# Seven block products for eight: Strassen's scheme in the down projection of a streaming encoder step

## The chip, the core and the metric

The kernel runs on one core of one Trainium2 chip. The metric is the device time of one execution in microseconds (us): 2781.47 us, the median of three runs (2781.33 to 2783.16).

## What is computed

One step of a hybrid encoder layer over 512 prompt tokens and 128 sample tokens (together 640 rows, five token tiles of 128), with model width 2048. The step is a long one (modulation, projections, attention, a recurrent branch, output projection, MLP); the change is in the last product of the MLP:

```python
x = x + gate_a * rmsnorm(mixed @ w_out, g_post_mix)
h = rmsnorm(x, g_pre_mlp) * (1 + scale_m) + shift_m
f = jnp.square(jax.nn.relu(h @ w_up)) @ w_down      # u = relu(.)^2, (640, 8192) ; w_down (8192, 2048)
return x + gate_m * rmsnorm(f, g_post_mlp)
```

All inputs are fp32. Every matrix product is made of three matmuls on fp32r operands: an operand is split into a high part and the rest (`hi`, `lo`), and hi\*hi + hi\*lo + lo\*hi is summed.

## The kernel before

The program is laid out by a tile scheduler: the code is written in program order with priorities (`tc.high_priority(200)` for splits and weight loads), pools give the buffers, and the scheduler fixes one order of instructions per engine. Each engine then works through its own list in order, and an instruction that waits holds back all behind it. DMAs are issued by SyncE (SP), also in order.

A split (`split_into`, L83 to L86) is one ScalarE (ACT) cast to `hi` (L85) and one VectorE (DVE) subtraction for `lo` (L86). Weights arrive as half blocks of 128x1024 fp32 (512 KB) in a ring of six buffers (tag `raw`), and their `hi` and `lo` lie in three buffers each (`PARTS = 3`).

The MLP's first product (`up_pair`, L993 to L1037) already goes by Strassen's scheme: seven products of 24 matmuls for two column tiles, with weight sums on DVE ahead of some splits (L1010, L1016, L1026, L1032). Its result u goes to DRAM, transposed, in 64 tiles `u_dr[f]` of 128 x 640.

The down projection starts at L1054. `acc` (128 x 5 x 2048, fp32) holds the result in SBUF. K = 8192 is cut into 16 blocks n of 512, the 2048 columns into four column blocks cb of 512. For each n, four tiles of u are read back and split (`up_tile`, tags `fh`, `fl`, five buffers each); for each cb the two half blocks of `w_down[n, cb]` are loaded and split, and for each of five token tiles t (`down_cols`, L1066 to L1077) 12 matmuls (4 tiles of u, 3 of hi and lo) go into one PSUM bank, which DVE then adds to `acc` (L1077; L1075 is the copy for n = 0). So one (n, cb) is 60 matmuls, two splits and five additions. The last block, n = 15, is kept apart: its weights are split into `late_h`, `late_l`, and norm, gate and output of each token tile follow its matmuls.

AH and AL are two SBUF areas (tags of the pool `act`) of 128 x 10240 fp32. In the up projection they hold the operands of its products; in the down projection they are free until `late_h` and `late_l`.

Of the kernel before, what the change touches and what calls it, by code (L numbers as in the profile page):

```python
# [19 lines left out]
P = 128  # L20
# [19 lines left out]
def stream_step(ctx: ExitStack, tc: tile.TileContext, I, O):  # L40
# [86 lines left out]

    u_dr = [dr.tile([P, T], F32, name=f"u_dr{f}") for f in range(64)]

# [600 lines left out]
    with tc.tile_pool(name="ph2", bufs=1) as pl:  # L730
# [169 lines left out]
        def up_out(c, f, half, op):  # L900

            V.scalar_tensor_tensor(out=c, in0=c, scalar=0.0, in1=c, op0=op, op1=ALU.mult)
            nc.sync.dma_start(u_dr[f][:, H2 * half : H2 * half + H2], c)

# [36 lines left out]
        def plain(j, ct, half):  # L941
# [11 lines left out]
            S.activation(c, c, AF.Square)  # L953
            nc.sync.dma_start(u_dr[2 * j + ct - 1][:, H2 * half : H2 * half + H2], c)
            yield
# [35 lines left out]
    with tc.tile_pool(name="up", bufs=1) as pl:  # L991
# [3 lines left out]
        def up_pair(j):  # L995
# [40 lines left out]
            S.activation(c, c, AF.Square)  # L1036
            nc.sync.dma_start(u_dr[2 * j][:, H2:], c)  # L1037

# [13 lines left out]


    with tc.tile_pool(name="ph3", bufs=1) as pl:  # L1054
        acc = pl.tile([P, NT, D], F32, name="acc")
        NBLK = 16

        def up_tile(f):
            with tc.high_priority(200):
                u = load(u_dr[f], f"u{f}")  # L1060
            fh = pl.tile([P, T], F32R, tag="fh", bufs=5, name=f"fh{f}")
            fl = pl.tile([P, T], F32R, tag="fl", bufs=5, name=f"fl{f}")
            split_into(fh, fl, u)
            return fh, fl

        def down_cols(n, fs, t, cb, parts, ps):  # L1066
            for kk in range(4):
                xh, xl = [x[:, P * t : P * t + P] for x in fs[kk]]
                wh, wl = cols(parts, 512 * kk, 512)
                PE.matmul(ps, xh, wh, start=kk == 0, stop=False)  # L1070
                PE.matmul(ps, xh, wl, start=False, stop=False)  # L1071
                PE.matmul(ps, xl, wh, start=False, stop=kk == 3)  # L1072
            dst = acc[:, t, 512 * cb : 512 * cb + 512]
            if n == 0:
                V.tensor_copy(dst, ps)  # L1075
            else:
                V.tensor_add(dst, dst, ps)  # L1077
# [11 lines left out]
        n = NBLK - 1  # L1089
        fs += [up_tile(4 * n + i) for i in (1, 2, 3)]  # L1090
        first = load_split(I["w_down"][n, 0], f"d{n}0")
# [28 lines left out]
        for t in range(NT):  # L1120
            down_cols(n, fs, t, 0, first, bank("s", f"dn{n}0{t}"))
        gate = [None] * 4
# [12 lines left out]
        for i, t in enumerate(order):  # L1135
            for cb in range(1, 4):
                down_cols(n, fs, t, cb, late[cb], bank("sto"[(3 * t + cb) % 3], f"dn{n}{cb}{t}"))
# [107 lines left out]
```

## Time and profile before

| what | before |
|---|---|
| median of 3 runs | 2781.47 us |
| the profiled execution | 2785.3 us, of which 2783.2 us span |
| PE (TensorE) busy | 2720.8 us, 98% |
| DVE busy | 1481.9 us, 53% |
| ACT busy | 951.0 us, 34% |
| down projection, first to last matmul | 1890.6 to 2771.7 us |

The page gives busy time by engine, then the costliest groups of instructions with the duration of one and the idle time ahead of it; the trace behind it can be asked for single stretches. A matmul's duration in the trace (390 ns) is longer than its distance to the next one, because matmuls overlap; what counts is the number in a stretch in which PE never rests. The same holds, less strongly, for DVE: an instruction that waits for nothing starts a little before the one ahead of it has ended. Names: `dn` is a bank of the down projection, `d_h`, `d_l` the split weights, `fh`, `fl` the split u.

### The profile page before, as it was taken

The numbers are of one execution on the slowest core, as the hardware profiler recorded it, in microseconds if no ns is written. First come the engines' busy times: TensorE is split into PE (matmuls) and PEld (weight loads), VectorE is DVE, ScalarE is ACT, GpSimd is POOL, SyncE is SP. The second block draws the span as 40 slices with busy tenths as digits, with TensorE's granted clock in tenths as the row PEclk, the third lists the DMA queues.
The fourth block names the chain that finished last, engine by engine and source line by source line (L and its number), as shares of the span: only waits on it lengthen the run. The fifth ranks groups of instructions, "written<-read, shape, count | busy, mean of one in ns | idle before, by whom it ended". The sixth has DMA issues, their size and how long they took to land.

```text
span 2783.2 us, 39612 instructions
## 1 busy us (share of the span) xinstructions
PE 2720.8 (98%) x15934; PEld 2331.2 (84%) x15934; DVE 1481.9 (53%) x2377; ACT 951.0 (34%) x1530; POOL 53.2 (2%) x103
## 2 busy tenths in 40 slices
PE   7999999999999989999999999999999999999998
PEld 3677787877768778899999999997888888888886
DVE  5465534435353366766666666664444544444457
ACT  4264433433353255433333333332211211121222
POOL 0000000000000011100000000000000000000000
PEclk9999999999999999999999999999999999999999
DMA  9944465665664466733333333333333332232235
GB/s 335 352 148 153 153 201 182 212 212 188 227 212 144 161 247 224 234 105 116 111 118 110 115 107 117 110 110 104 121 94 96 109 110 92 95 122 89 92 117 178
DMA packets 148279, 425.92 MB, mean 153 GB/s; under 512 B 21976, under 2 KB 48504, under 8 KB 145536
## 3 DMA queue, kind: packets, MB, share of 16 engines
q1 hardware_dynamic: 143824, 406.28, 44.3%
q0 software_dynamic: 4128, 17.04, 1.7%
q8 instruction: 125, 2.05, 0.3%
q14 instruction: 58, 0.48, 0.1%
q10 hardware_dynamic: 144, 0.07, 0.0%
HBM read 375.94 MB, written 47.40 MB: 152 GB/s over the span
## 4 chain that ended last, share of the span: by engine, by line
PE 91%; DMA 3%; issue 2%; ACT 2%; DVE 2%; POOL 0%; SPq 0%; DVEq 0%; ACTq 0%; POOLq 0%
PE dn L1071 10%; PE dn L1070 10%; PE dn L1072 10%; PE u L895 8%; PE u L896 8%; PE u L897 8%; PE wo L757 2%; PE wo L759 2%; PE wo L758 2%; PE mm_ps L142 2%; PE g_ps L142 1%; PE zx L211 1%; PE zg L211 1%; PE ma_ps L142 1%; PE zx L213 1%
## 5 line engine op out<-in xcount | busy, mean ns | idle before, releaser
L1070 PE MATMUL dn<-d_h,fh 128*128 128x512 f32 x1220 | 473.7, 390 | 5.9 <-ACT fh L85 4.4
L1071 PE MATMUL dn<-d_l,fh 128*128 128x512 f32 x1220 | 475.5, 391 | 0.0
L1072 PE MATMUL dn<-d_h,fl 128*128 128x512 f32 x1220 | 473.4, 390 | 0.0
L1077 DVE TENSOR_TENSOR acc<-acc,dn 128x512 f32<-128x512 f32 x300 | 205.8, 686 | 321.8 <-PE dn L1072 319.2
L85 ACT CAST d_h<-d_r 128x1024 fp32r<-128x1024 f32 x122 | 127.9, 1048 | 512.9 <-PE dn L1072 503.1
L1070 PEld LDWEIGHTS dn<-d_h,fh 128*128 128x128 f32 x1220 | 229.6, 188 | 54.7 <-ACT fh L85 4.7
L1071 PEld LDWEIGHTS dn<-d_l,fh 128*128 128x128 f32 x1220 | 229.5, 188 | 51.7 <-DVE d_l L86 4.2
L1072 PEld LDWEIGHTS dn<-d_h,fl 128*128 128x128 f32 x1220 | 229.5, 188 | 47.5 <-DVE fl L86 0.4
L86 DVE TENSOR_TENSOR d_l<-d_r,d_h 128x1024 fp32r<-128x1024 f32 x122 | 148.9, 1221 | 85.4 <-ACT d_h L85 85.4
L758 PE MATMUL wo<-wo_l,mix_hi 128*128 128x512 f32 x320 | 125.8, 393 | 1.4 <-DVE wo_l L86 1.4
L757 PE MATMUL wo<-wo_h,mix_hi 128*128 128x512 f32 x320 | 126.6, 396 | 0.0
L759 PE MATMUL wo<-wo_h,mix_lo 128*128 128x512 f32 x320 | 125.7, 394 | 0.0
L86 DVE TENSOR_TENSOR wo_l<-wo_r,wo_h 128x1024 fp32r<-128x1024 f32 x48 | 58.6, 1223 | 104.3 <-ACT wo_h L85 101.5
L85 ACT CAST fh<-u 128x640 fp32r<-128x640 f32 x64 | 43.9, 725 | 145.9 <-PE dn L1071 144.0
L86 DVE TENSOR_TENSOR a_l<-u,a_h 128x1024 fp32r<-128x1024 f32 x41 | 50.2, 1225 | 71.4 <-ACT a_h L85 71.4
L85 ACT CAST wo_h<-wo_r 128x1024 fp32r<-128x1024 f32 x48 | 50.1, 1051 | 111.7 <-PE wo L759 99.6
L757 PEld LDWEIGHTS wo<-wo_h,mix_hi 128*128 128x128 f32 x320 | 60.6, 190 | 16.4 <-issue 3.6
L211 PE MATMUL zg<-h_hi,zg_h 128*128 128x320 f32 x224 | 73.9, 330 | 0.0
L211 PE MATMUL zx<-h_hi,zx_h 128*128 128x320 f32 x224 | 73.7, 329 | 0.0
L895 PE MATMUL u<-mix_hi,g_h 128*128 128x320 f32 x232 | 71.8, 309 | 1.6 <-DVE p L1028 1.6
L758 PEld LDWEIGHTS wo<-wo_l,mix_hi 128*128 128x128 f32 x320 | 60.6, 190 | 13.8 <-DVE wo_l L86 1.8
L897 PE MATMUL u<-mix_hi,g_l 128*128 128x320 f32 x232 | 71.7, 309 | 0.0
(1730 smaller groups left out, 6647.5 us busy)
## 6 DMA issues: line engine op xcount, KB each, us to landing
u<-in_w_up_dram SPq DMA_DIRECT2D x140, 512.0 KB
d_r<-in_w_down_dram SPq DMA_DIRECT2D x122, 512.0 KB
ma<-in_w_mod_dram SPq DMA_DIRECT2D x64, 512.0 KB
mm<-in_w_mod_dram SPq DMA_DIRECT2D x64, 512.0 KB
g<-in_w_mod_dram SPq DMA_DIRECT2D x64, 512.0 KB
wo_r<-in_w_out_dram SPq DMA_DIRECT2D x48, 512.0 KB
u<-u_dr SPq DMA_DIRECT2D x64, 320.0 KB
u_dr<-c SPq DMA_DIRECT2D x87, 160.0 KB
```

Of the source, the lines that this page charges most:

```text
L85: S.copy(hi, raw)
L86: V.tensor_sub(lo, raw, hi.bitcast(F32))
L211: PE.matmul(out, lh, AH[:, k, t], start=first, stop=False)
L757: PE.matmul(ps, xh, wh, start=first, stop=False)
L758: PE.matmul(ps, xh, wl, start=False, stop=False)
L895: PE.matmul(out, hi[:, c], xh[:, k, :], start=first and k == 0, stop=False, skip_group_check=True)
L896: PE.matmul(out, hi[:, c], xl[:, k, :], start=False, stop=False, skip_group_check=True)
L897: mm = PE.matmul(out, lo[:, c], xh[:, k, :], start=False, stop=k == 7, skip_group_check=True)
L1070: PE.matmul(ps, xh, wh, start=kk == 0, stop=False)
L1071: PE.matmul(ps, xh, wl, start=False, stop=False)
L1072: PE.matmul(ps, xl, wh, start=False, stop=kk == 3)
L1077: V.tensor_add(dst, dst, ps)
```

## The change

Blocks n = 0 to 14 are taken in eight groups: group 0 is block 0 alone, with its 512 values of K cut in two; groups 1 to 7 are pairs of blocks (n, n + 1), each of which is one half of K. The 512 prompt tokens are cut into two halves of 256, and the columns into the block cb and the block cb + 2. A group makes two passes (`columns`, cb = 0 and 1). In each pass, seven products (1, 2, 5, 6, 3, 7, 4, in this order) take the place of the eight of a two by two block product, on sums and differences of blocks of u and of w_down (Winograd's form). A product is, for each half h of its K (two in groups 1 to 7, one in group 0), 12 matmuls: two token tiles, two K tiles, three of hi and lo. The sample's token tile is not part of the scheme: its products are four more, 6 matmuls per h each, beside products 1, 2, 3 and 7 and on their split weights. Each product's banks are added to or subtracted from `acc` by `gather`; a bank goes on accumulating over several products.

The operands made of u are split into AH and AL (`ud_hi`, `ud_lo`, one set). During pass 1 of a group `u_operands` builds the next group's: seven of 128 x 1024 and three for the sample of 128 x 512 (in group 0 half as wide). Blocks of u are read through two buffers (`ar`) and one (`at`). u lies in DRAM in 16 tiles of 128 x 4 x 640.

```diff
-    u_dr = [dr.tile([P, T], F32, name=f"u_dr{f}") for f in range(64)]
+    u_dr = [dr.tile([P, 4, T], F32, name=f"u_dr{n}") for n in range(16)]
...
+        ORDER = (1, 2, 5, 6, 3, 7, 4)
+        AX_h = act.tile([P, 8704], F32R, tag="AH", name="ud_hi")
+        AX_l = act.tile([P, 8704], F32R, tag="AL", name="ud_lo")
+        groups = [[((0, 0), (0, 1))]] + [[((n, h), (n + 1, h)) for h in range(2)] for n in range(1, NBLK - 1, 2)]
...
+        def u_operands(g):
+            one = lambda r, t, name: u_part(g, r, 256 * t, 256, "ar", f"{name}_{g}")
+            u_split(g, 1, one(0, 0, "a11"))
+            yield
+            u_split(g, 2, one(1, 0, "a12"))
+            yield
+            x = u_part(g, 1, 256, 256, "at", f"a22_{g}")
+            V.tensor_sub(x, x, one(0, 1, "a21"))
+            u_split(g, 5, x)
+            yield
+            V.scalar_tensor_tensor(out=x, in0=x, scalar=-1.0, in1=one(0, 0, "b11"), op0=ALU.mult, op1=ALU.subtract)
+            u_split(g, 6, x)
+            yield
+            a = one(1, 0, "b12")
+            V.scalar_tensor_tensor(out=a, in0=x, scalar=-1.0, in1=a, op0=ALU.mult, op1=ALU.subtract)
+            u_split(g, 3, a)
+            yield
+            a = one(0, 0, "c11")
+            V.tensor_sub(a, a, one(0, 1, "c21"))
+            u_split(g, 7, a)
+            x1, x2 = [u_part(g, r, TP, TS, "ar", f"s{r}_{g}") for r in range(2)]
+            u_split(g, -1, x1)
+            u_split(g, -2, x2)
+            V.tensor_sub(x2, x2, x1)
+            u_split(g, -3, x2)
+            yield
+            u_split(g, 4, one(1, 1, "b22"))
+            yield
...
+        def product(g, i, raws, banks, first, name, sample=None):
+            nh = len(raws)
+            for h in range(nh):
+                with tc.high_priority(200):
+                    hi, lo = split(raws[h], f"{name}{i}{h}")
+                for p in range(2):
+                    at = place(i, h).start + P * p
+                    for kk in range(2):
+                        xs = [x[:, at + 256 * kk : at + 256 * kk + P] for x in (AX_h, AX_l)]
+                        dot(banks[p], xs, hi, lo, kk, first and h == 0 and kk == 0, h == nh - 1 and kk == 1)
+                if sample:
+                    s, ps, s_first, s_last = sample
...
+        def columns(g, cb, building):
...
+            def more(a, b):
+                with tc.high_priority(200):
+                    for x, y in zip(a, b):
+                        V.tensor_add(x, x, y)
...
+            product(g, 1, w11, b1, True, nm, (-1, y1, True, False))
+            for p in range(2):
+                gather(p, cb, b1[p], 1)
+            done()
...
+            product(g, 2, w21, b3, True, nm, (-2, y1, False, True))
...
+            more(w11, w12)
+            product(g, 5, w11, b2, True, nm)
...
+            more(w11, w22)
+            product(g, 6, w11, b1, False, nm)
...
+            product(g, 3, w22, b2, False, nm, (-3, y2, True, False))
...
+            more(w12, w22)
+            w21 = [w_half(g, h, 1, cb, "raw", "v21") for h in hs]
+            product(g, 7, w12, b1, False, nm, (-1, y2, False, True))
...
+            more(w11, w21)
+            product(g, 4, w11, b1, False, nm)
...
+        for _ in u_operands(0):
+            pass
+        for g in range(len(groups)):
+            columns(g, 0, iter(()))
+            columns(g, 1, u_operands(g + 1) if g + 1 < len(groups) else iter(()))
...
-        fs = [up_tile(0)]
-        for n in range(NBLK - 1):
-            fs += [up_tile(4 * n + i) for i in (1, 2, 3)]
-            cur, fs = fs, [up_tile(4 * n + 4)]
-            for cb in range(4):
-                parts = load_split(I["w_down"][n, cb], f"d{n}{cb}")
-                for t in range(NT):
-                    down_cols(n, cur, t, cb, parts, bank("s", f"dn{n}{cb}{t}"))
```

What the change does to the engines' lists is seen at three places. In the rows below, a name such as `d2160_l` is the low part of the weights of group 2, pass 1, product 6, half 0; `w11_210` is the block w11 of group 2, pass 1, half 0; `dn501` is the bank of n = 5, cb = 0, t = 1.

SP, where the up projection ends, before (the last stores of u, then weights):

```order
L903 DMA u_dr63_180<-c12_31_17558 128x320
L72 DMA d00_r_1024_17694<-in_w_down_dram 128x1024
L903 DMA u_dr63_180<-p5_31_17527 128x320
L1037 DMA u_dr62_179<-c21_31_17652 128x320
L72 DMA d01_r_0_17774<-in_w_down_dram 128x1024
```

The same place after:

```order
L903 DMA u_dr15_132<-c12_31_17510 128x320
L903 DMA u_dr15_132<-p5_31_17479 128x320
L1038 DMA u_dr15_132<-c21_31_17604 128x320
L1138 DMA w11_000_17668<-in_w_down_dram 128x1024
L1138 DMA w11_010_17842<-in_w_down_dram 128x1024
L1080 DMA a11_0_17616<-u_dr0_117 128x2x256
L1080 DMA a12_0_17620<-u_dr0_117 128x2x256
L1080 DMA a22_0_17624<-u_dr0_117 128x2x256
```

Before, the first tiles of u and the first two weight blocks are issued ahead of the last store (`c21_31`), in the rows shown and the ten above them; now the first weight block (`w11_000`) and the first blocks of u stand behind it, and the load of `w11_000` waits for that store's end, since its buffer lies where the up projection's pieces lay.

DVE in the middle of the stage, before (the end of n = 4 and the beginning of n = 5):

```order
L1077 TENSOR_TENSOR acc_17661<-acc_17661,dn433_19400 128x512
L86 TENSOR_TENSOR fl21_19431<-u21_19428,fh21_19430 128x640
L86 TENSOR_TENSOR fl22_19437<-u22_19434,fh22_19436 128x640
L1077 TENSOR_TENSOR acc_17661<-acc_17661,dn434_19414 128x512
L86 TENSOR_TENSOR d50_1_l_19461<-d50_r_1024_19454,d50_1_h_19460 128x1024
```

The same engine after, the splits of products 6 and 3 of group 2, pass 1 (`d2120`, `d2121` are the banks of product 5):

```order
L86 TENSOR_TENSOR d2160_l_19247<-w11_210_19082,d2160_h_19246 128x1024
L86 TENSOR_TENSOR ud_lo_17615<-a12_3_19195,ud_hi_17614 128x1024
L1173 TENSOR_TENSOR w11_210_19082<-w11_210_19082,v21_210_19339 128x1024
L86 TENSOR_TENSOR d2161_l_19263<-w11_211_19084,d2161_h_19262 128x1024
L1123 TENSOR_TENSOR acc_17613<-acc_17613,d2120_19199 128x512
L1123 TENSOR_TENSOR acc_17613<-acc_17613,d2121_19200 128x512
L1173 TENSOR_TENSOR w11_211_19084<-w11_211_19084,v21_211_19341 128x1024
L86 TENSOR_TENSOR d2130_l_19287<-w22_230_19144,d2130_h_19286 128x1024
```

Between two splits of weights there now stand a weight sum (L1173), a split of u for the group after (`ud_lo`) and the gathers (L1123).

DVE at the head of group 1, before (the end of n = 0 and the beginning of n = 1):

```order
L86 TENSOR_TENSOR d10_1_l_18053<-d10_r_1024_18046,d10_1_h_18052 128x1024
L86 TENSOR_TENSOR fl7_18035<-u7_18032,fh7_18034 128x640
L86 TENSOR_TENSOR fl8_18041<-u8_18038,fh8_18040 128x640
L1077 TENSOR_TENSOR acc_17661<-acc_17661,dn100_18056 128x512
L86 TENSOR_TENSOR d11_0_l_18131<-d11_r_0_18126,d11_0_h_18130 128x1024
```

The same place after, pass 0 of group 1, from the sixth operand to product 2's second half (`d1021_l`):

```order
L1098 SCALAR_TENSOR_TENSOR a22_1_17928<-a22_1_17928,b11_1_17954 128x1024
L1173 TENSOR_TENSOR w12_121_18119<-w12_121_18119,w22_121_18123 128x1024
L1102 SCALAR_TENSOR_TENSOR b12_1_17984<-a22_1_17928,b12_1_17984 128x1024
L86 TENSOR_TENSOR ud_lo_17615<-a22_1_17928,ud_hi_17614 128x1024
L86 TENSOR_TENSOR ud_lo_17615<-b12_1_17984,ud_hi_17614 128x1024
L1106 TENSOR_TENSOR c11_1_18017<-c11_1_18017,c21_1_18019 128x1024
L86 TENSOR_TENSOR ud_lo_17615<-c11_1_18017,ud_hi_17614 128x1024
L86 TENSOR_TENSOR ud_lo_17615<-s0_1_18024,ud_hi_17614 128x512
L86 TENSOR_TENSOR ud_lo_17615<-s1_1_18026,ud_hi_17614 128x512
L1111 TENSOR_TENSOR s1_1_18026<-s1_1_18026,s0_1_18024 128x512
L86 TENSOR_TENSOR d1021_l_18148<-w21_101_18069,d1021_h_18147 128x1024
```

For group 1 the operands' rows, from the first (`a11_1`, eleven rows further up) on, stand within its own pass 0, ahead of the second half of product 2, and not beside the pass before, as in the later groups.

## Rows read from the trace of the kernel before

**Rows 1.** The page: the span, and busy time of each engine.

```profile
span 2783.2 us, 39612 instructions
PE 2720.8 (98%) x15934; PEld 2331.2 (84%) x15934; DVE 1481.9 (53%) x2377; ACT 951.0 (34%) x1530; POOL 53.2 (2%) x103
```

**Rows 2.** Busy time by stretch: up projection, down projection, its end, its entry.

```profile
core 0: us, PE busy (x) PEld busy (x) DVE busy (x) ACT busy (x) POOL busy (x), PEclk, DMA share, GB/s
1200.00:1880.00 680.00, 680.00 (x4638) 680.00 (x4637) 442.68 (x466) 251.32 (x332) 0.00 (x0) 1.00 0.35 113
1950.00:2700.00 750.00, 750.00 (x3300) 618.04 (x3299) 353.87 (x440) 147.43 (x162) 0.00 (x0) 1.00 0.32 102
2700.00:2783.00 83.00, 70.62 (x309) 57.17 (x307) 58.84 (x100) 25.84 (x57) 0.00 (x0) 0.96 0.52 178
1884.00:1892.00 8.00, 3.59 (x18) 2.90 (x17) 2.68 (x3) 4.06 (x7) 0.00 (x0) 0.81 0.46 144
```

**Rows 3.** Waits from 2000 to 2700 us: who waited, total, times, longest.

```profile
ACT d_h L85 <- PE dn L1072: 434.8, 78, 11.2
DVE acc L1077 <- PE dn L1072: 292.5, 154, 2.0
DVE d_l L86 <- ACT d_h L85: 68.4, 39, 1.8
PEld dn L1071 <- DVE d_l L86: 3.9, 13, 0.3
```

**Rows 4.** The page's groups of instructions: busy, mean ns of one, idle before.

```profile
L1070 PE MATMUL dn<-d_h,fh 128*128 128x512 f32 x1220 | 473.7, 390 | 5.9 <-ACT fh L85 4.4
L1077 DVE TENSOR_TENSOR acc<-acc,dn 128x512 f32<-128x512 f32 x300 | 205.8, 686 | 321.8 <-PE dn L1072 319.2
L85 ACT CAST d_h<-d_r 128x1024 fp32r<-128x1024 f32 x122 | 127.9, 1048 | 512.9 <-PE dn L1072 503.1
L86 DVE TENSOR_TENSOR d_l<-d_r,d_h 128x1024 fp32r<-128x1024 f32 x122 | 148.9, 1221 | 85.4 <-ACT d_h L85 85.4
```

**Rows 5.** Timeline of PE at the entry: start, us, engine, line, instruction.

```profile
1890.57 0.80 PE L1070 MATMUL dn<-d_h,fh 128*128 128x512 f32 x1 [4.41 <-ACT fh L85]
1891.16 0.63 PE L1071 MATMUL dn<-d_l,fh 128*128 128x512 f32 x1
1891.59 0.63 PE L1072 MATMUL dn<-d_h,fl 128*128 128x512 f32 x1
...
1895.80 0.40 PE L1070 MATMUL dn<-d_h,fh 128*128 128x512 f32 x1
1896.03 0.39 PE L1071 MATMUL dn<-d_l,fh 128*128 128x512 f32 x1
```

**Rows 6.** The chain of waits at the entry, in order of time.

```profile
1887.84 1.78 DMA u_dr<-c
...
1889.79 0.73 ACT fh L85
```

**Rows 7.** Timeline of DVE in the up and the down projection.

```profile
1747.99 1.23 DVE L86 TENSOR_TENSOR a_l<-u,a_h 128x1024 fp32r<-128x1024 f32 x1 [2.25 <-ACT a_h L85]
1749.25 1.23 DVE L1010 TENSOR_TENSOR u<-u,u 128x1024 f32<-128x1024 f32 x1
1750.60 1.23 DVE L1026 TENSOR_TENSOR u<-u,u 128x1024 f32<-128x1024 f32 x1
...
2111.42 0.69 DVE L1077 TENSOR_TENSOR acc<-acc,dn 128x512 f32<-128x512 f32 x1
2112.02 1.22 DVE L86 TENSOR_TENSOR d_l<-d_r,d_h 128x1024 fp32r<-128x1024 f32 x1
2113.16 1.56 DVE L86 TENSOR_TENSOR fl<-u,fh 128x640 fp32r<-128x640 f32 x2
```

**Rows 8.** Timeline of SP and ACT: two weight loads issued, and the casts that awaited them.

```profile
1875.96 0.33 SPq L72 DMA_DIRECT2D d_r<-in_w_down_dram  x1
1881.93 0.33 SPq L72 DMA_DIRECT2D d_r<-in_w_down_dram  x1
...
1879.60 1.05 ACT L85 CAST d_h<-d_r 128x1024 fp32r<-128x1024 f32 x1 [4.60 <-DMA d_r<-in_w_down_dram]
1885.93 1.05 ACT L85 CAST d_h<-d_r 128x1024 fp32r<-128x1024 f32 x1 [5.28 <-DMA d_r<-in_w_down_dram]
1886.88 0.43 ACT L1035 ACTIVATE c<-u 128x320 f32<-128x320 f32 x1
```

**Rows 9.** The page: what the DMA engines moved in each of 40 slices.

```profile
GB/s 335 352 148 153 153 201 182 212 212 188 227 212 144 161 247 224 234 105 116 111 118 110 115 107 117 110 110 104 121 94 96 109 110 92 95 122 89 92 117 178
```

More of the change, by code (lines that the diff above doesn't have):

```diff
@@ new lines, in stream_step, with place, u_part @@
+        AX_h = act.tile([P, 8704], F32R, tag="AH", name="ud_hi")
+        AX_l = act.tile([P, 8704], F32R, tag="AL", name="ud_lo")
+        groups = [[((0, 0), (0, 1))]] + [[((n, h), (n + 1, h)) for h in range(2)] for n in range(1, NBLK - 1, 2)]
+        def place(i, h):
+            if i > 0:
+                return slice(1024 * ORDER.index(i) + 512 * h, 1024 * ORDER.index(i) + 512 * h + 512)
+            return slice(7168 - 512 * (i + 1) + 256 * h, 7168 - 512 * (i + 1) + 256 * h + 256)
+        def u_part(g, r, t0, w, tag, name):
+            x = pl.tile([P, len(groups[g]), 2, w], F32, tag=tag, bufs=1 if tag == "at" else 2, name=name)
+            if len(groups[g]) == 2:
+                nc.sync.dma_start(x.rearrange("p h k q -> p (h k) q"), u_dr[groups[g][0][r][0]][:, :, t0 : t0 + w])
+            else:
+                n, h = groups[g][0][r]
+                nc.sync.dma_start(x[:, 0], u_dr[n][:, 2 * h : 2 * h + 2, t0 : t0 + w])
+            return x.rearrange("p h k q -> p (h k q)")
@@ new lines, in u_split @@
+        def u_split(g, i, x):
+            c = slice(place(i, 0).start, place(i, 0).start + x.shape[-1])
+            split_into(AX_h[:, c], AX_l[:, c], x)
+        def u_operands(g):
[26 more added lines that the diff above has]
+            yield
@@ new lines, in stream_step, with gather, w_half @@
+        begun = set()
+        def gather(t, cb, ps, sign):
+            dst = acc[:, t, 512 * cb : 512 * cb + 512]
+            with tc.high_priority(100):
+                if (t, cb) in begun:
+                    (V.tensor_add if sign > 0 else V.tensor_sub)(dst, dst, ps)
+                elif sign > 0:
+                    V.tensor_copy(dst, ps)
+                else:
+                    V.tensor_scalar(dst, ps, -1.0, None, op0=ALU.mult)
+            begun.add((t, cb))
+        def w_half(g, h, r, cb, tag, name):
+            n, q = groups[g][h][r]
+            src = I["w_down"][n, cb][:, 1024 * q : 1024 * q + 1024]
+            with tc.high_priority(200):
+                if tag == "raw":
+                    return load(src, f"{name}_{g}{cb}{h}")
+                w = pl.tile([P, 1024], F32, tag=tag, bufs=4, name=f"{name}_{g}{cb}{h}")
+                nc.sync.dma_start(w, src)
+                return w
@@ new lines, in dot @@
+        def dot(ps, xs, hi, lo, kk, first, last):
+            c = slice(512 * kk, 512 * kk + 512)
+            PE.matmul(ps, xs[0], hi[:, c], start=first, stop=False, skip_group_check=True)
+            PE.matmul(ps, xs[0], lo[:, c], start=False, stop=False, skip_group_check=True)
+            PE.matmul(ps, xs[1], hi[:, c], start=False, stop=last, skip_group_check=True)
+        def product(g, i, raws, banks, first, name, sample=None):
[10 more added lines that the diff above has]
+                    s, ps, s_first, s_last = sample
+                    at = place(s, h).start
+                    for kk in range(2):
+                        xs = [x[:, at + P * kk : at + P * kk + P] for x in (AX_h, AX_l)]
+                        dot(ps, xs, hi, lo, kk, s_first and h == 0 and kk == 0, s_last and h == nh - 1 and kk == 1)
@@ new lines, in stream_step @@
+        for _ in u_operands(0):
[3 more added lines that the diff above has]
+            columns(g, 1, u_operands(g + 1) if g + 1 < len(groups) else iter(()))
+        n = NBLK - 1
+        fs = []
+        for t in range(NT):
+            u = raw_tile([P, 4, P], f"u15_{t}")
+            nc.sync.dma_start(u, u_dr[n][:, :, P * t : P * t + P])
+            x = pl.tile([P, 2, 4, P], F32R, tag=("at", "ar", "ar", "wl", "wl")[t], bufs=(1, 2, 2, 4, 4)[t], name=f"fs{t}")
+            split_into(x[:, 0], x[:, 1], u)
+            fs.append(x)
@@ L1120, in stream_step @@
         for t in range(NT):
-            down_cols(n, fs, t, 0, first, bank("s", f"dn{n}0{t}"))
+            down_cols(t, 0, first, bank("s", f"dn{n}0{t}"))
         gate = [None] * 4
```

61 lines of the change are left out of this document (39 added, 22 removed).

## The prediction

> **What bounds the kernel now.** I read the page's first section, then stretches, then waits. PE is busy 98% of the span [rows 1], but a busy PE proves little, so the stretch of the down projection is next: from 1950 to 2700 us PE is busy all 750 us, at granted clock 1.00, with 3300 matmuls [rows 2]. That is 227.3 ns for each, and the stage is PE's. The others wait for it: DVE's additions and ACT's casts waited 292.5 and 434.8 us for PE, PE's weight loads 3.9 us for DVE [rows 3]. DVE is busy 354 of the 750 us, ACT 147, the DMA engines 32% [rows 2]. The only hole is the entry: PE stood idle for 4.41 us, then ran its first twelve matmuls 0.43 us apart, until 1895.80 [rows 5].
>
> The profiled execution took 2785.3 us (span 2783.2 and 2.1 around it), 3.8 above the median of 2781.47. I sum against 2785.3 and take 3.8 off at the end.
>
> **Matmuls taken away.** Before, 15 blocks by 4 column blocks by 60 are 3600. After, the halves of K are 15 (one in group 0, two in each of seven groups); each costs, per pass, 7 products by 12 and 4 sample products by 6, so 108. 15 by 2 by 108 is 3240. The other 240, of block 15, stay. The form is the same (128x128 stationary, 512 columns [rows 4]), so each costs the same 227.3 ns: 360 by 0.2273 = **81.8 us less** wherever PE stays fed. Below that it can't go, as PE has no idle time in the stretch to give back.
>
> **What DVE gets.** A 1024-wide row takes 1.22 us and a 512-wide one 0.69 [rows 4], but the next row starts earlier: 1.14 us after a 1024-wide split, 0.60 after an addition [rows 7]. A row that waits for DVE's own previous one starts 1.26 to 1.35 after it [rows 7]. A pass of a pair has 14 splits, 8 weight sums and 16 gathers: 22 by 1.14 and 16 by 0.60, 34.7 us, beside 216 matmuls, 49.1 us. The operands of u add 11 rows of 1024 and 4 of 512, 14.9 us per group. In the order, a pass 1 that builds them (group 2) holds 31 and 16 rows, 44.9 us, and the next pass 0 24 and 20, 39.4 us. So DVE goes from 47% of the stage to 92% and 80% of PE's time. The up projection, by the same scheme, ran with DVE at 443 of 680 us and PE never idle [rows 2].
>
> A rule of the Trainium skill is set against this. By the rows, a row lets the next one start 0.08 to 0.09 us before its own end [rows 7]. The skill's page "VectorE: DVE Perf Modes", section "The DRAIN you can't avoid", has it that the next operation doesn't start until the pipeline has emptied; by full durations the building pass would be 31 by 1.22 and 16 by 0.69, 48.9 us, as long as PE's 49.1, and every wait in it would reach PE: by that the term of 12 us below would be some 30, and the sum 2764. The start-to-start times of this trace decide, so I keep 44.9.
>
> **Building passes of groups 1 to 6.** The weights' `hi` and `lo` have three buffers. A split can begin when PE lets one go and takes a cast (1.05) and a subtraction (1.14), 2.2 us, while PE has two half products, 5.5 us: 3.3 us of slack for whatever else DVE holds. Following the rows of one such pass with the durations above, the splits stay ahead through products 1, 2 and 5 and are closest at product 6's second half and product 3's first, 1 to 2 us ahead. Against that stands a21, which can be loaded only when operand 1 is split, since its buffer is one of two. A weight load of the same size took 3.64 and 4.00 us from issue to cast [rows 8], and DVE gets to a21 some 2.4 us after: it would wait 1 to 2 us with product 5's second split behind it. I take 2 us lost per building pass (0 if nothing slips, 6 if each of some twenty rows that wait costs 0.15 more and a21's wait passes through whole): 6 by 2 = **12 us**, between 0 and 36. The transfers behind it are covered: a pair moves 20 weight blocks of 0.52 MB and 5.2 MB of u in 98 us, 160 GB/s, and the DMA engines have done 352 [rows 9].
>
> **Entry.** Before: last store of u issued at 1887.84, done in 1.78; cast of `fh` at 1889.79 [rows 6]; PE at 1890.57 [rows 5]. After, the load of `w11_000` starts where that cast did, and takes 3.6 to 4.0 [rows 8]; two weight casts, 0.95 apart [rows 8], stand in ACT's list ahead of the first operand's, about 0.5. PE starts near 1895.8: **5 us** later (4 to 8). Its slow first dozen matmuls stay.
>
> **Group 0.** A product is one half, 24.5 us of PE per pass. DVE's rows in pass 0, from the first weight split to the last operand's, are 14 of 1024, 25 of 512 and 4 of 256 wide (0.33 by extension): 32.3 us, 7.8 more than PE's. The blocks a21, b12 and c21 each wait for a buffer that a split frees, adding 2 to 3 us: **10 us** (6 to 18). What is left for pass 1 fits (8 rows of 1024 and 13 of 512, 17 us).
>
> **Group 1.** Its operands aren't built in the pass before; in its pass 0 they stand between operand 1 and the second half of product 2: 15 rows of 1024 and 7 of 512, 21.3 us, plus some 3 us for c21, whose load waits for operand 3's split. PE has 36 matmuls (8.2 us) to do and then the sample's, whose operands come last. The run starts about when PE ends group 0, so PE is idle some 16 us and then, as at the entry, runs a dozen matmuls at 0.43 us [rows 5]: **18 us** (10 to 26).
>
> **End.** `late_h` and `late_l` take AH and AL back, so their 8 splits, 9.1 us of DVE, begin only after the last product, beside 60 matmuls (13.6 us): **1 us** (0 to 9). Before, this stretch had PE at 70.6 of 83 us [rows 2].
>
> **Sum.** 2785.3 - 81.8 + 12 + 5 + 10 + 18 + 1 = 2749.5; less 3.8 is **2746 us**. With all low ends 20 come back instead of 46, 2720; with all high ends 97, 2797.
>
> **Rivals.**
> - The head is hidden: operands overlap better than their order suggests, entry 4, group 0 3, group 1 5, passes 0, together 12: 2712 us. For it: PE may take matmuls of pass 1 early. Against: the loads in a row at group 0 and group 1's place in the list.
> - The gain is nearly eaten: all terms near their high ends, 2772 to 2788.
> - Slower: PE and DVE hold each other up in every pass. DVE works its list in order; a gather that awaits PE's bank, or an operand that awaits a load, holds back the split that PE needs next. One such standoff costs PE a cast, a subtraction and a gather, 2.8 us; two per pass over 14 passes are 78 us in place of the 12: 2812. It decides from 3.4 us per pass on, where the 36 us and the 12 are gone. For it: 92% of DVE in building passes and three buffers. Against: the up projection has the same chain and buffers without a wait, at 65%.
>
> **How the numbers follow.** A measurement of this kernel can tell about 0.2%, 5.6 us, from no change. Forecast 0.60 (2726 to 2772), head hidden 0.17, gain eaten 0.09, slower 0.14. Faster than 2775.9: the first two and half of the third, 0.81; within 0.2%: 0.05; slower 0.14. The range reaches from the hidden head to the eaten gain, 2710 to 2784, and leaves out the standoffs and a little below.
>
> **What would show it.** Right: 3240 matmuls in the seven products and the sample, 227 ns apart wherever PE is fed; DVE at 80 to 92% in the middle groups with PE's idle time there under 3% and mostly in building passes; one idle time of over 10 us in group 1, ended by an operand's split; the entry near 1896 after a load of w_down. Wrong: PE waiting in pass 0 of the middle groups too, for splits or gathers (the third rival); no long wait in group 1 (the first); DVE rows of 1024 starting 1.22 us or more apart where none waits.

## The result, and the profile after

The changed kernel takes 2754.47 us (median of four runs, 2746.72 to 2754.7) against 2781.59 before: a ratio of 0.9895 (95% interval 0.9877 to 0.9912), 27 us faster. The prediction was 2746, in a range of 2710 to 2784. The profiled execution of after took 2754.47 us, of which 2752.4 span, to be set against the 2783.2 of before [rows 1].

The page: span and busy time, then the three costliest groups of the stage.

```profile
span 2752.4 us, 39345 instructions
PE 2651.9 (96%) x15574; PEld 2271.7 (83%) x15574; DVE 1749.0 (64%) x2604; ACT 1075.0 (39%) x1641; POOL 53.2 (2%) x103
...
L1143 PE MATMUL d<-d_h,ud_hi 128*128 128x512 f32 x840 | 330.8, 394 | 23.7 <-ACT ud_hi L85 10.2
...
L1144 PE MATMUL d<-d_l,ud_hi 128*128 128x512 f32 x840 | 330.0, 393 | 2.8 <-DVE d_l L86 2.8
L1145 PE MATMUL d<-d_h,ud_lo 128*128 128x512 f32 x840 | 328.6, 392 | 1.8 <-DVE ud_lo L86 1.8
```

Three times 840 matmuls of the prompt and 720 of the sample's banks are the 3240 of the sum. 360 are gone from PE's count (15,934 to 15,574), and DVE has worked 267 us more.

Busy time by stretch (the columns as in [rows 2]): 75 us of group 2 in which PE never waits, its building pass (pass 1), the pass 0 behind it, and the end of the program.

```profile
2104.00:2179.00 75.00, 75.00 (x332) 61.76 (x330) 62.10 (x65) 28.81 (x29) 0.00 (x0) 1.00 0.54 172
2131.00:2181.00 50.00, 48.32 (x214) 39.69 (x212) 44.56 (x48) 21.28 (x21) 0.00 (x0) 1.00 0.56 179
2181.00:2231.00 50.00, 50.00 (x220) 41.18 (x221) 40.97 (x45) 16.73 (x17) 0.00 (x0) 1.00 0.44 137
...
2681.00:2752.00 71.00, 58.95 (x258) 47.88 (x256) 52.37 (x93) 22.39 (x53) 0.00 (x0) 0.95 0.49 172
```

Where PE is fed, 332 matmuls take 75 us, at granted clock 1.00: a matmul costs what it did. DVE is busy 89% and 82% of the two passes. All that PE waited for in the stage is in six rows (who waited, for whom, total, times, longest).

```profile
PE d10y L1143 <- ACT ud_hi L85: 16.7, 1, 16.7
PE d L1143 <- ACT ud_hi L85: 10.2, 1, 10.2
PE d L1143 <- DVE acc L1123: 9.6, 6, 2.4
PE d L1143 <- ACT d_h L85: 3.9, 4, 1.2
PE d L1144 <- DVE d_l L86: 2.8, 2, 2.1
PE d L1145 <- DVE ud_lo L86: 1.8, 2, 1.6
```

The first is the sample's operand in group 1, the second the entry, the third a wait for a gather at the first product of each of groups 2 to 7, the rest group 0. PE's timeline has the entry, the long wait, and one of the six:

```profile
1896.93 0.79 PE L1143 MATMUL d<-d_h,ud_hi 128*128 128x512 f32 x1 [10.17 <-ACT ud_hi L85]
...
1986.07 0.79 PE L1143 MATMUL d10y<-d_h,ud_hi 128*128 128x512 f32 x1 [16.71 <-ACT ud_hi L85]
...
2381.42 0.50 PE L1143 MATMUL d<-d_h,ud_hi 128*128 128x512 f32 x1 [1.82 <-DVE acc L1123]
```

**An account that closes.** From the first matmul of the stage (1896.93) to the first of the last block (2681.25) are 784.3 us: 3240 by 0.2273 are 736.5; PE's idle rows in it sum to 34.8; the remaining 13.1 are matmuls further apart than 0.2273, in stretches at a lower clock behind those waits (as in [rows 5]; after the longest one, from 1986.00 to 1991.00, the granted clock was 0.59). "Slow clock" stands for this loss below. Before, the same stretch was 1890.57 to 2711.76: 818.3 for the matmuls and 2.9 of slow clock. So of the 81.8 us that the matmuls give, 45.0 are given back inside the stage. Of the experiments this stretch is compared first: PE ended the up projection anywhere between 1880.9 and 1891.1 us in the traces here, with the same matmuls ahead, so whole times differ by several us for reasons that are not the change's.

### The profile page after: what moved, and what is told of

Its sections match the earlier page's. It is cut to its first block, busy times and chain, and to the rows that moved or that the text cites. A ratio compares the mean times of both kernels' runs of the same rounds, so it can differ in the third digit from the quotient of the medians.

```text
span 2752.4 us, 39345 instructions
## 1 busy us (share of the span) xinstructions
PE 2651.9 (96%) x15574; PEld 2271.7 (83%) x15574; DVE 1749.0 (64%) x2604; ACT 1075.0 (39%) x1641; POOL 53.2 (2%) x103
## 4 chain that ended last, share of the span: by engine, by line
PE 80%; DVE 10%; DMA 6%; issue 2%; ACT 2%; SPq 0%; POOL 0%; DVEq 0%; ACTq 0%; POOLq 0%
PE u L895 9%; PE u L896 9%; PE u L897 9%; PE d L1143 4%; PE d L1144 4%; PE d L1145 4%; PE wo L757 3%; PE wo L758 2%; PE wo L759 2%; DVE d_l L86 2%; DVE ud_lo L86 2%; DMA c<-u_dr 2%; PE mm_ps L142 2%; DVE acc L1123 1%; DMA u<-in_w_up_dram 1%
## 5 line engine op out<-in xcount | busy, mean ns | idle before, releaser
L85 ACT CAST d_h<-w 128x1024 fp32r<-128x1024 f32 x210 | 220.7, 1052 | 404.3 <-PE d L1145 112.8
L1143 PE MATMUL d<-d_h,ud_hi 128*128 128x512 f32 x840 | 330.8, 394 | 23.7 <-ACT ud_hi L85 10.2
L1144 PE MATMUL d<-d_l,ud_hi 128*128 128x512 f32 x840 | 330.0, 393 | 2.8 <-DVE d_l L86 2.8
L1145 PE MATMUL d<-d_h,ud_lo 128*128 128x512 f32 x840 | 328.6, 392 | 1.8 <-DVE ud_lo L86 1.8
L86 DVE TENSOR_TENSOR d_l<-w,d_h 128x1024 fp32r<-128x1024 f32 x210 | 255.5, 1222 | 92.3 <-ACT d_h L85 79.3
L1143 PEld LDWEIGHTS d<-d_h,ud_hi 128*128 128x128 f32 x840 | 158.7, 189 | 62.5 <-DVE acc L1123 14.1
L1144 PEld LDWEIGHTS d<-d_l,ud_hi 128*128 128x128 f32 x840 | 159.1, 189 | 36.9 <-DVE d_l L86 4.2
L1145 PEld LDWEIGHTS d<-d_h,ud_lo 128*128 128x128 f32 x840 | 159.1, 189 | 36.5 <-DVE ud_lo L86 3.5
L1123 DVE TENSOR_TENSOR acc<-acc,d 128x512 f32<-128x512 f32 x208 | 137.4, 682 | 7.7 <-PE d L1145 7.7
L1173 DVE TENSOR_TENSOR w<-w,w 128x1024 f32<-128x1024 f32 x90 | 109.3, 1221 | 0.7
```

Of the source, the lines that this page charges most:

```text
L1123: (V.tensor_add if sign > 0 else V.tensor_sub)(dst, dst, ps)
L1143: PE.matmul(ps, xs[0], hi[:, c], start=first, stop=False, skip_group_check=True)
L1144: PE.matmul(ps, xs[0], lo[:, c], start=False, stop=False, skip_group_check=True)
L1145: PE.matmul(ps, xs[1], hi[:, c], start=False, stop=last, skip_group_check=True)
```

## The experiments

Beside each time stands its ratio to the kernel before, run on the same chip. "Head" is what groups 0 and 1 lost in idle time and slow clock (with the pairs first, group 0 alone), "middle" what the groups behind them lost, both summed from PE's timeline as above; a wait where one building pass ends and the next pair begins counts with the middle.

| kernel | idle at entry | stage | head | middle | median | ratio to before (95%) |
|---|---|---|---|---|---|---|
| changed kernel | 10.2 | 784.3 | 33.8 | 14.0 | 2754.47 | 0.9895 (0.9877 to 0.9912) |
| the same again | 10.0 | 781.2 | 34.4 | 10.4 | 2753.13 | 0.9890 (0.9872 to 0.9907) |
| eight products | 10.0 | 852.1 | 33.5 | 0.3 | 2816.27 | 1.0110 (1.0092 to 1.0129) |
| c21 through `at` | 9.9 | 785.6 | 26.3 | 22.8 | 2752.33 | 0.9869 (0.9848 to 0.9889) |
| a21, c21 places of their own | 10.9 | 767.0 | 25.1 | 5.4 | 2737.42 | 0.9834 (0.9820 to 0.9847) |
| priority for group 1 | 10.1 | 781.5 | 28.1 | 16.9 | 2747.20 | 0.9862 (0.9848 to 0.9876) |
| first weight in `raw` | 9.8 | 779.1 | 28.7 | 14.0 | 2746.04 | 0.9859 (0.9845 to 0.9872) |
| those three together | 9.9 | 765.6 | 23.9 | 5.2 | 2731.53 | 0.9814 (0.9801 to 0.9828) |
| single block last | 11.6 | 772.6 | 25.7 | 10.4 | 2743.63 | 0.9853 (0.9838 to 0.9868) |
| last, own places, `raw` | 12.8 | 753.7 | 12.8 | 4.5 | 2723.97 | 0.9779 (0.9765 to 0.9793) |
| and the sample early | 13.3 | 751.5 | 9.3 | 5.7 | 2719.23 | 0.9766 (0.9750 to 0.9781) |
| and a11 in `raw` | 2.3 | 757.0 | 14.1 | 6.5 | 2721.37 | 0.9763 (0.9748 to 0.9779) |

### What one product is worth

```diff
+                again = 2 if i == 4 else 1
                 for p in range(2):
                     at = place(i, h).start + P * p
-                    for kk in range(2):
...
+                    for r in range(again):
+                        for kk in range(2):
...
```

> Product 4 of every pass is computed twice into the same banks, so that there are eight products of 24 matmuls (12 in group 0) again and 360 matmuls more in all, with no instruction more on any other engine; its result is not the reference's. If a matmul is worth 227.3 ns here, as before the change, PE gets 81.8 us more work, of which the waits at the starts of groups 2 to 7 (14.3 us with the slow clock behind them) are absorbed, since DVE gets 5.5 us more per pass: 2754.5 + 81.8 - 14.3 = 2822. If the waits are not DVE's lateness but a fixed price of changing from one group to the next, 2836. So this also says what the seventh-for-eighth is worth by itself, against the 81.8 us of the sum.

The stage takes 852.1 us for 3600 matmuls, 818.3 of them work, and the six waits have shrunk to three:

```profile
PE d L1143 <- DVE acc L1123: 1.4, 3, 1.0
```

The stage grew by 67.8, which is 81.8 less 14.0, what the middle of the changed kernel lost: the first of the two expectations. So 227.3 ns a matmul is what a product costs and gives, and the waits are no fixed price of changing groups: with 5.5 us more of PE's work per pass DVE catches up. The head lost 33.5 us, the changed kernel's 33.8: it isn't a matter of a few us of slack.

### What PE waits for at the start of each pair

The DVE timeline of the changed kernel, at the end of a building pass (group 4, then group 5), says what stood before the gather that PE awaited at 2379.6:

```profile
2374.40 1.23 DVE L1106 TENSOR_TENSOR c<-c,c 128x1024 f32<-128x1024 f32 x1 [2.09 <-DMA c<-u_dr]
2375.54 0.68 DVE L1123 TENSOR_TENSOR acc<-acc,d41y 128x512 f32<-128x512 f32 x1
2376.14 1.22 DVE L86 TENSOR_TENSOR d_l<-w,d_h 128x1024 fp32r<-128x1024 f32 x1
2377.28 1.22 DVE L86 TENSOR_TENSOR ud_lo<-c,ud_hi 128x1024 fp32r<-128x1024 f32 x1
2378.41 1.22 DVE L1173 TENSOR_TENSOR w<-w,w 128x1024 f32<-128x1024 f32 x1
2379.55 1.22 DVE L86 TENSOR_TENSOR d_l<-w,d_h 128x1024 fp32r<-128x1024 f32 x1
2380.68 0.68 DVE L1123 TENSOR_TENSOR acc<-acc,d 128x512 f32<-128x512 f32 x1
```

DVE waits 2.09 us for the load of c21; from there it works without a gap until the gather, and PE has waited 1.82. In the six groups it waited 11.2 us for c21 and 8.0 for a21 (from 2004 to 2681 us; who waited, total, times, longest):

```profile
DVE c L1106 <- DMA c<-u_dr: 11.2, 6, 2.7
DVE a L1095 <- DMA a<-u_dr: 8.0, 6, 2.0
```

The first try moved c21's load to the buffer that is free one operand earlier.

```diff
-            V.tensor_sub(a, a, one(0, 1, "c21"))
+            V.tensor_sub(a, a, u_part(g, 0, 256, 256, "at", f"c21_{g}"))
```

> One line differs from the changed kernel: c21, the block of u that is subtracted from c11, is read into the single buffer (at), which is free once operand 6 is split, instead of into one of the two buffers (ar), which it gets only when operand 3 is split. Theory A (a late load): in the changed kernel DVE waits 1.6 to 2.1 us for c21 at the end of every building pass, everything behind it in DVE's list comes that much later, and PE pays it at the first matmul of the next pair, 9.6 us in six waits, and 4.7 us of slow clock behind them. In group 1 the same wait is 5.1 us. Then PE's waits at the starts of groups 2 to 7 fall below 2 us in all, the one in group 1 from 16.7 to about 12, and the time from 2754.5 to about 2737. Theory B (DVE is simply full: 31 and 16 rows, 44.9 us, in a pass of 49.1): the lag comes back at another load or split, the six waits stay above 6 us in all, and the time stays above 2750.

In group 1 it did what was expected (the wait fell from 16.7 to 11.4), in the middle the opposite: 22.8 us lost instead of 14.0, and the whole time no better than the changed kernel's. The timelines of DVE, SP and PE in this variant show why:

```profile
2055.35 1.22 DVE L86 TENSOR_TENSOR ud_lo<-b,ud_hi 128x1024 fp32r<-128x1024 f32 x1
2060.74 1.23 DVE L1106 TENSOR_TENSOR c<-c,c 128x1024 f32<-128x1024 f32 x1 [4.17 <-DMA c<-u_dr]
2061.89 1.22 DVE L86 TENSOR_TENSOR d_l<-w,d_h 128x1024 fp32r<-128x1024 f32 x1
2063.02 1.28 DVE L1123 TENSOR_TENSOR acc<-acc,d 128x512 f32<-128x512 f32 x2
...
2054.33 0.52 SPq L1077 DMA_DIRECT2D c<-u_dr  x1
...
2063.85 0.77 PE L1143 MATMUL d<-d_h,ud_hi 128*128 128x512 f32 x1 [2.92 <-DVE acc L1123]
```

The scheduler, which expects c21 sooner, now puts its subtraction one split and two gathers earlier in DVE's list. The load was issued at 2054.33, the moment the buffer came free, and took 6.4 us to the row that awaited it; DVE stands 4.17 us instead of some 2, and the split and the gathers stand behind it. PE's waits are no longer at the starts of the pairs: all six, 14.5 us, now stand 24 matmuls ahead of one, at the last product of the building pass (product 4), which adds to the banks that those gathers read. DVE's waits in the same stretch:

```profile
DVE c L1106 <- DMA c<-u_dr: 22.0, 6, 4.5
DVE a L1095 <- DMA a<-u_dr: 8.1, 6, 1.9
```

The wait for c21 doubled and PE's waits grew with it, from 9.6 us to 14.5, while the wait for a21 stayed: that speaks for c21 as the one that reaches PE. Theory B's numbers came out, but by a longer wait for a load, so neither theory is decided by it. So the waits themselves were taken away, in 1024 of the 1536 columns that each of the operand areas AH and AL leaves unused:

```diff
+            if tag in ("h", "l"):
+                flat = (AX_h if tag == "h" else AX_l)[:, 8704 : 8704 + 512 * len(groups[g])].bitcast(F32)
...
-            V.tensor_sub(x, x, one(0, 1, "a21"))
+            V.tensor_sub(x, x, u_part(g, 0, 256, 256, "l", f"a21_{g}"))
...
-            V.tensor_sub(a, a, one(0, 1, "c21"))
+            V.tensor_sub(a, a, u_part(g, 0, 256, 256, "h", f"c21_{g}"))
```

> The blocks a21 and c21 get places of their own, in the unused ends of the operand areas (1024 columns each), so that their loads no longer wait for a split; the arithmetic is the same. Theory A (DVE's waits for these loads, with gathers behind them, make PE's waits): in the first trace of the changed kernel DVE waited 11.2 us for c21 and 8.0 for a21 in six groups, and 5.1 for c21 in group 1; without them PE's waits at the starts of groups 2 to 7 and the slow clock behind them, 14.0 us, fall below 4, the one in group 1 from 16.7 to about 11, and the stage takes 768 to 770 us instead of 784. Theory B (DVE is full whatever the loads do): the lag is made up of rows alone, the waits stay above 8 us, and the stage above 777.

The stage takes 767.0 us. From 2004 us on DVE waits neither for c21 nor for a21; what is left of PE's waits, from 2000 us on, is five of at most 1.1 us:

```profile
PE d L1147 <- DVE acc L1127: 4.3, 5, 1.1
```

Theory A holds, with a remainder: 5.4 us of the middle are left, above the 4 expected. That the stage came so near the expected 768 to 770 is partly chance, since the wait in group 1 fell further than foretold, to 8.9 us for 11. DVE still waits 8.6 us in five waits for a22, the block from which a21 is subtracted (its one buffer wasn't changed). With a21 in a place of its own, that row has moved a whole group forward in DVE's list, to the end of the building pass before its own, and PE's five waits are behind it, again at product 4:

```profile
2066.77 1.23 DVE L1099 TENSOR_TENSOR a<-a,ud_lo 128x1024 f32<-128x1024 f32 x1 [1.60 <-DMA a<-u_dr]
...
2069.88 0.47 PE L1147 MATMUL d<-d_h,ud_hi 128*128 128x512 f32 x1 [0.75 <-DVE acc L1127]
```

As a measure of the scatter, the changed kernel once more:

> The changed kernel once more, beside the runs below on the same chip. In its first trace PE began the stage at 1896.9 us, in four variants of it at 1891.0 to 1894.8, though all instructions ahead are the same; so the part ahead of the change should be seen to vary by several us between executions, while the stretch from the first matmul of the stage to the first of the last block stays at 784 us within 2.

The stage took 781.2, 1 us outside the expected 2, and began at 1892.7; its five times spread from 2746.3 to 2762.5. A difference of 3 us in the stage, or of 8 us in a single time, is thus no finding here.

### The head: the wait in group 1, and group 0

```diff
+        def soon(it):
+            while True:
+                with tc.high_priority(200):
+                    if next(it, it) is it:
+                        return
+                yield
...
-            columns(g, 1, u_operands(g + 1) if g + 1 < len(groups) else iter(()))
+            columns(g, 1, (soon(u_operands(g + 1)) if g == 0 else u_operands(g + 1)) if g + 1 < len(groups) else iter(()))
```

> Group 1's operands get the priority of the weights' splits, so that their rows stand in pass 1 of group 0 and not in pass 0 of group 1; nothing else differs from the changed kernel. Theory A (place in the list): pass 1 of group 0 leaves DVE some 7 us (17 us of its own rows beside 24.5 us of PE), so PE's wait for the sample's operand falls from 16.7 us to about 9 and the time from 2754.5 to about 2746. Theory B (one set of operands): operands can't be split before the products of pass 1 that read the old ones are done, so splits that group 0 needs now wait behind them; the wait in group 1 shrinks by less than 3 us or moves into group 0, and the time stays within 3 us of 2754.5 or rises.

The wait of 16.7 us is gone altogether, which neither theory had; in its place PE waits 6.4 us for gathers, around the same time. The head lost 28.1 us instead of 33.8: 6 of the 8 expected by theory A. But part of the wait did move, as B had it, since the operand rows now hold back what group 0 needs (group 0 alone loses some 23 us, 14.0 in the changed kernel), and the stage, 781.5 us, can't be told from the repeat's 781.2, as the middle happened to lose more.

```profile
PE d L1143 <- DVE acc L1127: 3.9, 2, 2.3
...
PE d L1143 <- DVE acc L1123: 2.6, 1, 2.6
```

Next, the first load of the stage:

```diff
-            w11 = [w_half(g, h, 0, cb, "wl", "w11") for h in hs]
+            w11 = [w_half(g, h, 0, cb, "wl" if g or cb else "raw", "w11") for h in hs]
```

> Group 0's first weight block (w11, pass 0) is read into the ring of raw buffers, which the up projection leaves free, instead of a buffer of the down projection's own, so its load is issued some 10 us ahead of the last store of u. Theory A (the entry is this load, then two casts): PE starts when a11 has been loaded and cast, near 1893.5 instead of 1896.9, and the time falls by 2 to 4 us. Theory B (a11, read behind the last store, would come at 1896 anyway, since five transfers share the DMA engines there): PE starts within 1 us of 1896.9 and the time doesn't move.

PE's idle time at the entry is 9.8 instead of 10.0 to 10.2: theory B on the start. Without the weight's load the block a11 behind the last store holds PE up just as long. The stage took 2 to 5 us less, at the edge of the scatter; group 0 lost 10.0 us, 14.0 in the changed kernel. There PE no longer waited for a low part of an operand (`ud_lo`, 1.8 us above): DVE had the first splits behind it when a11 came. All three edits together:

> Three edits together: the places of their own for a21 and c21, the priority for group 1's operands, and group 0's first weight block in the ring of raw buffers. If their gains add (14 in the middle groups by theory A of the first edit, 6 in groups 0 and 1 as the second edit showed alone and some 3 more without the load's wait, 4 in group 0 as the third showed alone), the stage falls from 784 to about 757 us and the time by some 27 us, to about 2727. If DVE is simply full, only the second and third count: 774 us and 2744.

765.6 us, against 767.0 with the own places alone: the other two add next to nothing, and 757 was wrong. PE now waits in pass 1 of group 0, for a copy that DVE reaches only behind three operand rows and a split of weights:

```profile
1942.82 1.22 DVE L1102 SCALAR_TENSOR_TENSOR a<-a,b 128x1024 f32<-128x1024 f32 x1
1943.95 1.22 DVE L86 TENSOR_TENSOR d_l<-w,d_h 128x1024 fp32r<-128x1024 f32 x1
1945.09 1.22 DVE L1106 SCALAR_TENSOR_TENSOR b<-a,b 128x1024 f32<-128x1024 f32 x1
1946.22 1.22 DVE L86 TENSOR_TENSOR ud_lo<-a,ud_hi 128x1024 fp32r<-128x1024 f32 x1
1947.36 0.68 DVE L1129 COPY acc<-d01y 128x512 f32<-128x512 f32 x1
```

```profile
PE d01y L1147 <- DVE acc L1129: 6.3, 1, 6.3
```

DVE runs there all but without a gap from 1930 to 1948. A pass of 24.5 us has no room for a pair's operands, wherever they stand in the list: 17 us of its own rows and 21.3 of theirs. So the short pass was moved away from a pair's front:

```diff
-        groups = [[((0, 0), (0, 1))]] + [[((n, h), (n + 1, h)) for h in range(2)] for n in range(1, NBLK - 1, 2)]
+        groups = [[((n, h), (n + 1, h)) for h in range(2)] for n in range(0, NBLK - 2, 2)] + [[((NBLK - 2, 0), (NBLK - 2, 1))]]
```

> The single block is taken last (block 14) and the pairs are (0, 1) to (12, 13); all else as in the changed kernel. Theory A (the loss in group 1 comes from a building pass of half length ahead of a pair): the wait of 16.7 us and its slow clock go, and the head has a pair to build: up to the sample's last operand 17 rows of 1024 and 5 of 512 on DVE, 22.4 us, and some 8 us of waits for loads, beside 8.2 us of matmuls: some 22 us lost in place of 12.7 in group 0 and 18.7 in group 1. The stage takes 772 to 780 us. Theory B (the first set of operands is the loss, wherever it stands, and a pair's is twice as long): 30 us lost at the head, and the stage stays at 784 or more.

772.6 us: theory A. 25.7 are lost at the head (22 expected), 16.8 of them in one wait for the sample's operand, and 10.4 in the middle, where the repeat of the changed kernel lost as much.

> The single block last, places of their own for a21 and c21, and the first weight blocks in the ring of raw buffers, together. With the single block last alone the head lost 22.7 us and the groups behind it 10.4; with the places of their own alone those lost 5.4. If the two are independent, the middle loses 5 us and the head, without its waits for a21 and c21, some 16: the stage takes about 758 us (767.0 and 772.6 with each alone), and the time is near 2727. If they hinder each other, as the priority did, it stays at 765 or more.

753.7: these do add, and better than expected (12.8 lost at the head, 4.5 behind). The wait for the sample's operand is 8.1 us. Then that operand was built earlier:

```diff
             u_split(g, 2, one(1, 0, "a12"))
+            if g == 0:
+                u_sample(g)
```

> As the run before, and for the first group alone the sample's three operands are built behind the second operand instead of behind the seventh. Theory A (the long wait at the first set of operands is the sample's place in the list: its first matmuls stand in PE's list behind product 1): the wait of 16.8 us for it, seen with the single block last, falls to 5 or less, later operands cost PE some 3 to 5 us as they come just in time, and the stage takes some 750 us. Theory B (DVE's rows of the whole first pass, 49.6 us beside 49.1 of PE, decide, in whatever order): the wait moves to products 5 to 7 and the stage gains less than 3 us on the run before.

The wait for the sample is gone, yet the stage has only 2.2 us less, within the scatter; 3.1 us have come back as waits for the copies of later products. The run doesn't decide between the two: the waits and the 751.5 us are as theory A had them, the small gain as theory B, since the run before had lost only 8.1 us at the sample and not 16.8. The three largest entries of PE's waits in this kernel:

```profile
PE d L1153 <- ACT ud_hi L85: 13.3, 1, 13.3
PE d L1153 <- DVE acc L1133: 4.1, 5, 1.1
PE d L1153 <- DVE acc L1137: 3.1, 3, 1.8
```

The first is the entry, the largest wait left.

```diff
-            u_split(g, 1, one(0, 0, "a11"))
+            u_split(g, 1, one(0, 0, "a11") if g else u_part(g, 0, 0, 256, "raw", "a11_0"))
```

> As the run before, and the very first block of u (a11 of the first group) too is read into the ring of raw buffers, ahead of the last store of u. Theory A (PE's idle time at the entry is the transfer behind the last store, since the down projection's own buffers lie where the up projection's pieces lay): PE's idle time ahead of the stage falls from 10 us to 3 or 4, and since the second operand and the sample's still come behind that store, half of it is given back: 3 us less in all, counted from the end of the up projection. Theory B (the operand areas are held by the up projection to its end, and a cast, a split and the first matmuls' low clock follow in any case): the idle time stays above 8 us.

PE's last matmul of the up projection, then the first of the stage:

```profile
1889.80 0.31 PE L897 MATMUL u<-mix_hi,g_l 128*128 128x320 f32 x1
1892.37 0.78 PE L1156 MATMUL d<-d_h,ud_hi 128*128 128x512 f32 x1 [2.26 <-ACT ud_hi L85]
```

The idle time falls from 13.3 to 2.3 us, as theory A had it: what held the entry was a load behind the last store. The stage takes 5.5 us more, since the second operand still comes behind that store (5.15 us of waiting). From the end of the up projection that is 5.5 us less, but the times of the two kernels, 2719.23 and 2721.37, can't be told apart. The last three kernels beat both the kernel before the change and the changed one: 2719 us is 0.9766 of before (0.9750 to 0.9781), and the 27 us of the change have become 67 (2785.95 less 2719.23, on one chip).

## Why the prediction came out as it did

The trace gives each term of the sum its own number, against the stretches of before, and they add up to what the span lost (2783.2 to 2752.4):

| term | predicted | measured |
|---|---|---|
| 360 matmuls | -81.8 | -81.8 |
| building passes, groups 1 to 6 | +12 | +14.0 (9.6 idle, 4.4 slow clock) |
| entry | +5 | +5.8 (10.17 idle, 4.41 before) |
| group 0 | +10 | +11.1 (7.8 idle, 6.2 slow clock, less 2.9 before) |
| group 1 | +18 | +19.8 (17.4 idle, 2.4 slow clock) |
| end | +1 | -0.3 (71.15 us, 71.44 before) |
| end of the up projection | 0 | +0.6 |
| span | -35.8 | -30.8 |

- **The matmuls** held exactly, and the eighth product confirmed them from the other side.
- **Building passes:** the size was right, the mechanism half wrong. The prediction looked for PE's waits within the pass, at the splits of products 6 and 3, behind a wait for a21. Inside the passes of the changed kernel PE never waited. DVE did wait for a21 (8.0 us in six), and the pass swallowed it; what reached PE was the wait for c21 near the pass's end, which has no time left to make it up, paid at the next pair's first product, for the gather that frees its bank. The run with c21 alone moved and the one with both blocks in places of their own show this. And only 9.6 us were idle time: the slow clock behind it, 4.4 us, had no part in the term. c21 wasn't in the working for these passes, though it was named for group 1. The prediction listed waits in pass 0 of the middle groups as a sign of its third rival. They came, at one place per pair, 0.6 to 2.4 us each, not two of 2.8 us per pass: the form of the standoff was that rival's, its size an eighth of its 78 us (9.6; with the slow clock 14.0, under a fifth).
- **A load's time was mis-sized.** 3.64 and 4.00 us [rows 8] were for weights. c21, of the same size, took 5.6 us from its issue (2068.19) to the row that awaited it in the changed kernel, 6.4 in the variant through `at` (2054.33 to 2060.74).

```profile
2068.19 0.52 SPq L1077 DMA_DIRECT2D c<-u_dr  x1
...
2073.80 1.23 DVE L1106 TENSOR_TENSOR c<-c,c 128x1024 f32<-128x1024 f32 x1 [1.56 <-DMA c<-u_dr]
```

In group 1 the "some 3 us for c21's load" were 5.1, in group 0 the first weight load itself, issued with others behind the last store, took 4.66 us (1889.71 to 1894.37).

- **Group 1** came as foretold, 16.7 us idle for 16, ended by the sample's operand, but the size was partly luck. The sum had 21.3 us of rows and 3 of waiting. PE went on from the first of the sample's three operands and not from the last, so from the first operand's row (1959.75) to that one 26.3 us passed, some 18.6 of them rows and 7.7 waits: 5.07 for c21 and 2.6 for ACT's casts, which the sum hadn't.

```profile
1980.99 1.23 DVE L1106 TENSOR_TENSOR c<-c,c 128x1024 f32<-128x1024 f32 x1 [5.07 <-DMA c<-u_dr]
1983.32 1.23 DVE L86 TENSOR_TENSOR ud_lo<-c,ud_hi 128x1024 fp32r<-128x1024 f32 x1 [1.11 <-ACT ud_hi L85]
1986.05 0.69 DVE L86 TENSOR_TENSOR ud_lo<-s,ud_hi 128x512 fp32r<-128x512 f32 x1 [1.50 <-ACT ud_hi L85]
```

That the operands' place in DVE's list makes it was right for this kernel; but the place alone could not be bettered, since the single block's pass is too short (the priority's runs). Moving that pass to the end did.

- **Entry and group 0:** right within 1.1 us each. That the entry is the transfer behind the last store was shown by the last run (2.3 us). But the prediction had PE wait for the first weight's load and two casts of weights ahead of the operand's, and without them the idle time was still 9.8 us: a11, read behind the same store, comes no sooner. In group 0 the fit is partly luck. 7.8 us were idle, less than the 10 foretold; the 3.3 us of slow clock beyond that of before weren't in the term. The first weight's lateness, which the term hadn't either, had a part in it (10.0 us lost with that weight in `raw`). What share DVE's rows have in the rest no run shows.
- **The rule on DVE's rows:** in the DVE rows of the changed kernel above, a 1024-wide row starts 1.13 to 1.14 us after the one before it where none waits (2376.14, 2377.28, 2378.41, 2379.55), and lasts 1.22. Its sum of 30 us for the building passes, drawn from the Trainium skill, page "VectorE: DVE Perf Modes", section "The DRAIN you can't avoid" (the next operation starts only when the pipeline has emptied), isn't borne out: 14.0 were lost, and only 5.4 with the loads of a21 and c21 out of the way. The section itself adds that a next operation that is not held starts earlier, and these rows agree, 0.08 to 0.09 us before the end of the one ahead.
- **From the profiled time to the median** the prediction took 3.8 us off. The changed kernel's profiled execution lay at its median. With the 5.0 by which the terms together were too low this is all of the distance between forecast (2745.7 before rounding) and result, 8.8 us. The part ahead of the change varies by up to 10 us between traces here, so one profiled execution doesn't give a constant offset; what varies there was not looked into.

## What to carry to other kernels

When a change takes work from the bound engine and gives it to a second one, fill the second one's list pass by pass: at 89% of a pass it made up 1.3 us of waiting for a load in mid pass and passed on 2 us near the end. Loads that an in-order list awaits want a buffer of their own, for a buffer that comes free a little sooner also moves the waiting row forward in the list, in front of work that was on time. And a stage that prepares the next step beside the present one should not begin with a short step.

## What was not expected of the hardware

- A wait of PE can cost more than its length: behind 34.8 us of idle time the stage lost another 13.1, most of it to matmuls 0.43 us apart (0.23 otherwise). One wait of 1.82 us, in group 5, was followed by 1.8 us of it, one of 1.87 in group 4 by 0.2. Behind the first the granted clock averaged 0.62, most of that stretch at the lower of its two levels (1.2 and 2.4 GHz); behind the second it stayed at 1.00 (the columns as in [rows 2]). What decides between the two stays open.

```profile
2281.20:2284.00 2.80, 2.77 (x12) 2.31 (x13) 2.80 (x4) 0.62 (x1) 0.00 (x0) 1.00 0.21 32
2382.70:2387.00 4.30, 4.30 (x13) 3.39 (x12) 3.15 (x4) 0.00 (x0) 0.00 (x0) 0.62 0.44 122
```

- Two transfers of 0.52 MB, a block of u and a block of weights, differed by 1.6 to 2.8 us from issue to first use (c21 here, 5.6 and 6.4; the weights of [rows 8], 3.64 and 4.00). Which part of that is the blocks' shape in DRAM and which the transfers beside them stays open.
